# Eight plain products for the first feature tile of each FFN, a table written in eight pieces, and a queue clock in the emitter

## The chip, the cores and the metric

The kernel runs on one core of a Trainium2 chip. The metric is device time in microseconds (us). Five engines take part: TensorE (PE: matmuls, and weight loads that overlap them, PEld), VectorE (DVE), ScalarE (ACT), GpSimd (POOL) and SyncE (SP), which here only issues transfers. A transfer issued by SP goes to queue q1, one issued by POOL to q0; both use the same 16 DMA engines.

## The reference

One decoder layer over 1032 tokens (a prompt of 1024 and 8 single sample tokens), width 1024, in float32:

```
h <- LN1(alpha*h + 0.5*SwiGLU_1(h))            w_up 1024 x 5632, w_down 2816 x 1024
h <- LN2(alpha*h + merge(window attention(h), retention(h)) W_o)
h <- LN3(alpha*h + 0.5*SwiGLU_2(h))
SwiGLU(x) = (silu(x W_gate) * (x W_up)) W_down
```

The attention adds a relative-position bias to its scores; the kernel builds that table once. Both feed-forward networks (FFN 1 and FFN 2) have the same shape.

## The kernel before

**Precision.** A float32 operand is split in a high part (rounded to fp32r by a copy on ACT) and a low part (the rest, a subtraction on DVE). A product is three matmuls: high by high, high by low, low by high. For weights these are `w_hi` and `w_lo`, for tokens the two halves of the tiles `T`.

**Up stage.** FFN features are cut into 22 tiles `ft` of 128. For one tile the gate and the up weights are two row blocks; with two halves of the 1024 inputs they form a 2 x 2 block matrix, the tokens in two halves of 516 (columns) form another: b11, b21 are the input halves of the first 516 tokens (in `ya`, `yb`), b12, b22 those of the last. The kernel multiplies them in the Strassen-Winograd way: seven products (ft, 0) to (ft, 6) in place of eight. Each product is 4 k-steps x 3 parts x 2 column chunks = 24 matmuls of 258 columns. It needs sums of weight blocks (four additions on DVE in `sums`, into the tiles `st`) and sums of token blocks. The token operands T0 to T6 are made once for each FFN by `t_stage`: T0 = b11, T1 = b21 and T5 = b22 are plain (two ACT copies, two DVE subtractions); T2, T3, T4 and T6 are differences, each with two more DVE subtractions ahead, done in place in `ya` and `yb`, so that their order is bound. In the first seven steps of an FFN these operands are made while the products run. Products are accumulated in three PSUM pairs pr0 to pr2 (`pr`); `evac_p` empties them: copies on ACT, additions on DVE into the tiles `a`, then the gate (a tanh on ACT into `th`, then (th+1)*a on DVE), the product of gate and up part in `m`, its split in `ah` and `m`, and two stores to DRAM (`adr`).

Before, the first two tiles are interleaved: (0,0), (1,0), (0,1), (1,1), then (0,3), (0,2), (0,4), (0,5), (0,6), then the rest of tile 1, in FFN 1. In FFN 2, (0,0), (0,1), (1,0), (1,1) come first, which need only T0 and T1, while the last layer norm (`ln_last`) still works on the tokens from 768 on; `end_ln` waits for it.

**Down stage.** Features come back from DRAM in groups (`fetch_one`, transfers T<-adr of 1 MB); the first six are issued while the last up tile runs. A job is one 128 x 1024 row block of weights (two halves of 256 KB), used in 6 or 12 units over three token chunks. A unit's PSUM bank (`mb`, four in turn) is added to `ya` or `yb` by DVE.

**Weights.** Halves are loaded by SP in one fixed order into four buffers `raw`; the buffer is reloaded (`load`) once its last reader was issued. Eight slots hold split weights (`NSLOT`). `prep` issues the split of one half; `prep_ahead` calls it ahead of need, while slots are free and the half should have arrived by the emitter's clock.

**Order.** All instructions of an engine run in the order in which the program issues them. The emitter `E` keeps a model time for PE (`E.pe`) and for each other engine; `E.later` holds a piece of work until its model time; generators (side tasks) are resumed at model times; `need` issues a prep at once; while `env["busy"]` is set, `prep_ahead` does nothing. Model times set the order, nothing on the chip waits for them. A load's arrival by the model is

```
arrive[h] = E.pe + DMA_T          # DMA_T = 2.8
```

**Bias table.** `bias_tables` makes 8 rows of 256 values and writes each 128 times to DRAM with one POOL transfer (`scr<-rsb`, 8 x 128 x 256 values, 1 MB); the attention reads it back from 765 us on.

Of the kernel before, what the change touches and what calls it, by code (L numbers as in the profile page):

```python
# [40 lines left out]
DMA_T = 2.8  # L41
# [20 lines left out]
class Emit:  # L62


    def __init__(self, nc):
        self.nc = nc
        self.pe = 0.0
        self.eng = {"act": 0.0, "dve": 0.0, "pool": 0.0}
# [144 lines left out]
def build(tc, I, O):  # L213
# [3 lines left out]
    with ctx:  # L217
# [90 lines left out]
        def open_sa():  # L308
            p = ctx_open("sa", R)
            env["st"] = [p.tile([P, 4, P], F32, name=f"st{i}") for i in range(3)]  # L310
            env["a"] = [p.tile([P, HT], F32, name=f"a{i}") for i in range(4)]

        def open_ut():
            p = ctx_open("ut", L)
            env["th"] = p.tile([P, HT], F32, name="th")
# [28 lines left out]
        def ffn_units(p, r0):  # L344
# [12 lines left out]
            if p:  # L357
                pre = 2 * len(wrow)
                wrow.append(up[1])
                halves[pre] = halves[pre + 1] = 1  # L360
                src = {(1, 0): (pre, None), (1, 1): (pre + 1, None)}
            else:
                src = {(1, 0): (-1, None), (1, 1): (-2, None)}
            for ft in range(NF):
                h = 2 * len(wrow)
                wrow.extend((up[ft], up[ft] + 1))
                for k, n in enumerate((1, 1, 1, 2) if ft == 1 else (2, 2, 1, 2)):
                    halves[h + k] = n
# [6 lines left out]
            units.extend(dict(kind="P", p=p, c=0, ft=ft, i=i, jobs=[]) for ft, i in order)  # L375
# [46 lines left out]
        for ui, u in enumerate(units):  # L422
            u["ops"] = [quad_op[u["p"], u["ft"], u["i"]]] if u["kind"] == "P" else [o + i for o in (job_op[j] for j in u["jobs"]) for i in range(2)]
            for o in u["ops"]:
                lastu[o] = ui
# [42 lines left out]
        def prep():  # L468
# [6 lines left out]
            else:  # L475
                loaded(src)
                x = env["first"][-1 - src] if src < 0 else raw[src % NRAW]
# [4 lines left out]
            def lo():  # L482
                E.tt(w_lo[s], x, f(w_hi[s]), ALU.subtract, n=512)
                lo_of.pop(o, None)
                if not isinstance(src, str) and src >= 0:
                    used(src)
# [255 lines left out]
        env["first"] = [env["a"][i][:, 0:512].rearrange("p (k c) -> p k c", k=4) for i in (1, 3)]  # L742

        def first_half(t, row, h):
            ds(out=t, in_=half(I["w"][row].rearrange("p (k c) -> p k c", k=KD), h))

        for k in range(2):
            first_half(raw[k], wrow[0], k)
            for i in (0, 2):
                ds(out=env["yb" if k else "ya"][:, i:i + 2], in_=xd[:, 4 * k + i:4 * k + i + 2])  # L750
            first_half(env["first"][k], wrow[2], k)
        for h in range(4):
            arrive[h] = 0.0
            if h > 1:
                first_half(raw[h], wrow[1], h)
# [17 lines left out]
        def t_stage(i):  # L773
# [18 lines left out]
            elif i == 5:  # L792
                t_hl(5, b22)
            else:
                t_hl(6, sub(b11, b21, b11))

        def end_t(p):
# [6 lines left out]
            for fn in env.pop("held"):  # L804
# [26 lines left out]
        def start_u(p):  # L831
            env["held"] = []
            if p == 1:
                t_stage(1)
# [5 lines left out]
                env["a"] = [p.tile([P, HT], F32, name=f"a{i}") for i in range(2)] + [None] * 2  # L840
                open_pairs((1, 0, 2))

        def end_ln():

            E.force(list(lng.values()))
            env["a"][2:] = [env["ln"][:, i * HT:i * HT + HT] for i in (0, 1)]
            env["th"] = env["ln"][:, 2 * HT:3 * HT]

        def start_d(p):
# [8 lines left out]
            ds(out=env["ya"], in_=hres if p else xd[:, 0:4, :])  # L858
            alpha(env["ya"])
# [7 lines left out]
        def fetch_one():  # L867
# [3 lines left out]
            fstate["t"] = E.pe  # L871

# [34 lines left out]
        def bias_tables():  # L907
# [13 lines left out]
            dq(out=dst, in_=rsb.unsqueeze(1).to_broadcast([8, P, 256]))  # L921
# [361 lines left out]

        def evac_p(p, ft, i, bank):
            A = bank[:, :, 0:HC]
            v = lambda t: t.rearrange("p (c n) -> p c n", c=2)
            a1, a2, a5 = env["a"][ft % 2], env["a"][2], env["a"][3]

            def hold(fn):
                if "held" in env:  # L1290
                    env["held"].append(fn)
                else:
                    fn()

            def gate(a):

                def fn():
                    t = E.act(env["th"], a, AF.Tanh, scale=0.5, n=HT, after=E.eng["dve"])
                    env["glu"] = E.later(t, lambda: E.stt(a, env["th"], 1.0, a, ALU.add, ALU.mult, n=HT))

                hold(fn)

            if i in (0, 2, 3):
                E.act(v((a1, None, a2, a5)[i]), A, n=HT)
            elif i == 1:
                E.tt(v(a1), A, v(a1), ALU.add, n=HT)
                if ft != 1:
                    gate(a1)
            elif i == 4:
                E.tt(v(a5), A, v(a5), ALU.add, n=HT)  # L1310
                if "held" not in env:
                    E.do(env["glu"])
            elif i == 5:
                hold(lambda: E.do(env["glu"]))
                E.tt(v(a2), A, v(a2), ALU.add, n=HT)
                gate(a2)
            else:
# [4 lines left out]
                if ft == 0:  # L1322
                    gate(env["a"][1])
                t = E.act(ah, m, n=T, after=t)

                def lo():
                    t = E.tt(m, m, f(ah), ALU.subtract, n=T)

                    def out():
                        ds(out=adr[p, ft, :, 0:T], in_=f(ah))  # L1330
                        ds(out=adr[p, ft, :, T:2 * T], in_=m)

# [5 lines left out]
        def evac(u, bank):  # L1338
            kind, c = u["kind"], u["c"]
            n0, N = CH[c]  # L1340
            ps = None if kind == "P" else bank[:, :N]
            if kind == "P":
                evac_p(u["p"], u["ft"], u["i"], bank)
            elif kind == "down":
# [132 lines left out]
        def before(ui, u):  # L1477
            kind, c = u["kind"], u["c"]
            if kind == "P":
                p, ft, i = u["p"], u["ft"], u["i"]  # L1480
                o = u["ops"][0]
                if (ft, i) == (0, 0):
                    start_u(p)
                    if p:
                        for n in range(4):
                            need(o + n)
# [5 lines left out]
                    env["busy"] = True  # L1492
                    env["aside"] = lambda: (need(o + 4), need(o + 5))
                elif not p and (ft, i) == (1, 0):
                    need(o + 1)
                    t_stage(1)
                elif not p and (ft, i) == (1, 1):
                    need(o)
                    need(o + 1)
                elif ft == 0 and i > 1:  # L1500
                    if p and i == 3:
                        end_ln()
                        t_stage(3)
                    need(o)
                    if i < 6:
                        t_stage({3: 2, 2: 4, 4: 5, 5: 6}[i])
                    else:
                        end_t(p)
                        env["busy"] = False
                if ft == 0 and i in tready:  # L1510
                    E.pe = max(E.pe, tready.pop(i))
# [41 lines left out]
        def product(u, bank):  # L1553

            o = u["ops"][0]
            need(o)
            s, x = slot_of[o], TT[u["i"]]
            fresh = u["i"] in (0, 1, 3)
            for k in range(4):
                wh, wl = w_hi[s][:, k, :], w_lo[s][:, k, :]  # L1560
                for n, (w, lo) in enumerate(((wh, 0), (wh, 2 * T), (wl, 0))):
                    for c in range(2):
                        a = lo + k * HT + c * HC
# [182 lines left out]
```

## Time and profile before

| | |
|---|---|
| median of three runs | 2272.85 us (2272.41 to 2273.28) |
| profiled execution, own time | 2270.69 us |
| its span, first to last instruction | 2268.9 us |
| mean granted TensorE clock | 0.980 |
| DMA over the span | 254.88 MB, mean 112 GB/s |

In a timeline each line is: start, duration, engine, line of the kernel, instruction, output<-input, shape, count; in brackets the idle time of that engine just before, and what ended it. `raw<-in_w_dram` is a weight half, `T<-adr` a fetch of stored features, `w_hi` and `w_lo` are the parts of a split weight. A clock below 1.00 in a stage means that TensorE was granted less than its full clock there. Line 105 is the helper of all DVE operations, 101 of all activations, 83 of all matmuls.

### The profile page before, as it was taken

How to read it: one execution, taken by the hardware profiler on the slowest of the kernel's cores; microseconds unless marked ns; L12 is line 12 of the kernel's file. 1: busy time of each engine (PE TensorE's matmuls, PEld its weight loads, DVE VectorE, ACT ScalarE, POOL GpSimd, SP SyncE). 2: the span in 40 equal slices, each digit the busy share in tenths (PEclk: the TensorE clock that was granted, in tenths of full speed). 3: DMA queues.
4: the chain of work that ended last, by engine and by line, in shares of the span. 5: the costliest groups of instructions: out<-in, count | busy, mean ns of one | idle time of the engine just before them, and what ended most of it. 6: DMA issues, size and time to landing. Idle time of an engine off the chain costs nothing.

```text
span 2268.9 us, 38235 instructions
## 1 busy us (share of the span) xinstructions
PE 2169.8 (96%) x15333; PEld 2134.0 (94%) x15333; DVE 1377.2 (61%) x2575; ACT 772.8 (34%) x1481; POOL 227.9 (10%) x283
## 2 busy tenths in 40 slices
PE   6899999989999899999999999987999999989996
PEld 5899999989999889999989999987999999989996
DVE  7666666654334887555665847778666666543337
ACT  4343433321111576111233434544434434311113
POOL 1100000001002444111110201011000000010003
PEclk9999999999999999999999999998999999999998
DMA  3522332266330210111154344532223322484212
GB/s 124 130 102 102 112 108 104 94 235 259 122 103 28 64 41 30 47 39 39 57 178 144 131 130 131 186 108 84 102 101 113 108 104 100 173 316 145 85 42 75
DMA packets 105571, 254.88 MB, mean 112 GB/s; under 512 B 13370, under 2 KB 17170, under 8 KB 98978
## 3 DMA queue, kind: packets, MB, share of 16 engines
q1 hardware_dynamic: 104546, 251.36, 32.0%
q0 software_dynamic: 848, 1.09, 0.5%
q8 instruction: 120, 1.97, 0.4%
q14 instruction: 57, 0.47, 0.1%
HBM read 196.00 MB, written 57.45 MB: 112 GB/s over the span
## 4 chain that ended last, share of the span: by engine, by line
PE 79%; DVE 10%; DMA 5%; ACT 2%; issue 2%; POOL 1%; SPq 0%; DVEq 0%; POOLq 0%; ACTq 0%
PE mb L83 41%; PE pr L83 36%; DMA raw<-in_w_dram 5%; DVE w_lo L105 2%; PE sb L83 2%; DVE ya L105 1%; DVE T L105 1%; DVE yb L105 1%; DVE ln L105 1%; DVE zt L105 1%; ACT w_hi L101 1%; DVE rt L105 1%; ACT T L101 0%; POOL pt L121 0%; PE sb L91 0%
## 5 line engine op out<-in xcount | busy, mean ns | idle before, releaser
L83 PE MATMUL mb<-T,w_hi 128*128 128x384 f32 (+1 forms) x3936 | 930.8, 324 | 14.2 <-DVE yb L105 14.2
L83 PE MATMUL pr<-T,w_hi 128*128 128x258 f32 x4928 | 809.3, 287 | 35.6 <-ACT w_hi L101 12.9
L83 PEld LDWEIGHTS pr<-T,w_hi 128*128 128x128 f32 x4928 | 691.3, 192 | 41.1 <-ACT w_hi L101 14.4
L83 PEld LDWEIGHTS mb<-T,w_hi 128*128 128x128 f32 x3936 | 680.3, 189 | 20.2 <-DVE yb L105 15.1
L83 PE MATMUL mb<-T,w_lo 128*128 128x384 f32 (+1 forms) x1968 | 632.4, 321 | 0.0
L83 PE MATMUL pr<-T,w_lo 128*128 128x258 f32 x2464 | 504.2, 286 | 9.3 <-DVE w_lo L105 9.0
L101 ACT ACTIVATE w_hi<-raw 128x512 fp32r<-128x512 f32 x498 | 303.1, 624 | 478.0 <-PE mb L83 424.6
L105 DVE TENSOR_TENSOR w_lo<-raw,w_hi 128x512 fp32r<-128x512 f32 x498 | 350.9, 729 | 125.6 <-ACT w_hi L101 124.8
L83 PEld LDWEIGHTS pr<-T,w_lo 128*128 128x128 f32 x2464 | 389.4, 192 | 11.4 <-DVE w_lo L105 11.4
L83 PEld LDWEIGHTS mb<-T,w_lo 128*128 128x128 f32 x1968 | 372.1, 189 | 0.0
L105 DVE SCALAR_TENSOR_TENSOR yb<-mb,yb 128x384 f32<-128x384 f32 (+1 forms) x144 | 73.5, 514 | 136.3 <-PE mb L83 136.0
L105 DVE SCALAR_TENSOR_TENSOR ya<-mb,ya 128x384 f32<-128x384 f32 (+1 forms) x144 | 74.1, 515 | 134.3 <-PE mb L83 134.1
L101 ACT ACTIVATE w_hi<-st 128x512 fp32r<-128x512 f32 x132 | 82.5, 628 | 116.0 <-PE pr L83 59.6
L105 DVE TENSOR_TENSOR a<-pr,a 128x516 f32<-128x516 f32 x88 | 61.2, 696 | 99.5 <-PE pr L83 99.4
L125 POOL TENSOR_SCALAR ya<-ya 128x384 f32<-128x384 f32 (+1 forms) x24 | 11.6, 483 | 871.1 <-DMA ya<-hres 449.6
L105 DVE TENSOR_TENSOR w_lo<-st,w_hi 128x512 fp32r<-128x512 f32 x132 | 86.9, 684 | 0.0
L101 ACT ACTIVATE th<-a 128x516 f32<-128x516 f32 x44 | 28.0, 635 | 122.4 <-DVE a L105 121.6
L101 ACT ACTIVATE a<-pr 128x516 f32<-128x516 f32 x88 | 52.8, 601 | 40.4 <-PE pr L83 40.3
L105 DVE TENSOR_TENSOR ln<-pr,ln 128x516 f32<-128x516 f32 x44 | 30.6, 695 | 54.0 <-PE pr L83 54.0
L83 PE MATMUL mb<-o_hi,w_hi 128*128 128x384 f32 (+1 forms) x192 | 61.9, 322 | 0.0
L83 PE MATMUL mb<-g_lo,w_hi 128*128 128x384 f32 (+1 forms) x192 | 61.4, 320 | 0.0
L83 PE MATMUL mb<-g_hi,w_lo 128*128 128x384 f32 (+1 forms) x192 | 61.2, 319 | 0.0
(316 smaller groups left out, 2069.8 us busy)
## 6 DMA issues: line engine op xcount, KB each, us to landing
raw<-in_w_dram SPq DMA_DIRECT2D x502, 256.0 KB, 2.9
T<-adr SPq DMA_DIRECT2D x44, 1032.0 KB, 6.5
adr<-ya SPq DMA_DIRECT2D x44, 516.0 KB, 2.7
adr<-ah SPq DMA_DIRECT2D x22, 516.0 KB, 3.1
adr<-m SPq DMA_DIRECT2D x22, 516.0 KB, 4.1
out_yp_dram<-zt SPq DMA_DIRECT2D x16, 256.0 KB, 2.0
ya<-in_x_dram SPq DMA_DIRECT2D x2, 1032.0 KB, 8.9
yb<-in_x_dram SPq DMA_DIRECT2D x2, 1032.0 KB
```

Of the source, the lines that this page charges most:

```text
L83: self.nc.tensor.matmul(out=out, lhsT=lhsT, rhs=rhs, start=start, stop=stop, **kw)
L101: self.nc.scalar.activation(out=out, in_=in_, func=func, scale=scale, **kw)
L105: getattr(self.nc.vector, fn)(**kw)
L125: self.nc.gpsimd.tensor_scalar(out=out, in0=a, scalar1=s, scalar2=1.0, op0=ALU.mult, op1=ALU.mult)
```

## The change

It has three parts.

1. The first feature tile of each FFN is computed by eight plain products without weight sums. They stand in four units of kind "C", each of two products accumulated in one PSUM pair: C0 (gate, first token half: T0 and T1), C1 (up, first half: T0, T1), C2 (gate, second half: b12 and b22), C3 (up, second half). b12 gets an operand of its own (`t_stage(7)`, in the buffer that later holds T6); T5 is b22. The order is C0, C1, (1,0), (1,1), C2, C3, (1,3), (1,2), (1,4), (1,5), (1,6), then tile 2, in both FFNs. The differences are staged from C1 on in FFN 1, from C3 on in FFN 2. The four weight halves of tile 0 keep their slots from C0 to C3. `evac_c` empties the units: a copy, a gate, or a product with the gated tile; the split and the store of tile 0 wait (`held_ut`) until the buffers are free, and gates in FFN 2 wait (`held_th`) for `end_ln`. A fifth tile `a` is added, and `th` moves. The two weight halves of tile 1 that were loaded an additional time for the interleaving are loaded once.
2. The bias table is written by eight POOL transfers of 128 KB, one after another, 8 us of model time apart.
3. The emitter has a clock of the load queue: each load of a half (0.262 MB), fetch and store (1.057 MB) and the reload of the residual (2.114 MB) adds its size at 0.38 MB/us. A half's arrival is the later of that clock and of DVE's model time, plus 2.0 us.

The diff, cut to its core:

```
-DMA_T = 2.8
+DMA_T = 2.0
+DMA_R = 0.38
...
+    def dma(self, mb):
+        self.queue = max(self.queue, self.pe) + mb / DMA_R
+        return self.queue + DMA_T
...
-            order = [(0, 0), (0, 1), (1, 0), (1, 1)] if p else [(0, 0), (1, 0), (0, 1), (1, 1)]
-            order += [(0, i) for i in (3, 2, 4, 5, 6)]
-            order += [(ft, i) for ft in range(NF) for i in range(7) if (ft, i) not in order]
...
+            order = [(1, 0), (1, 1)]
+            order += [(1, i) for i in (3, 2, 4, 5, 6)]
+            order += [(ft, i) for ft in range(2, NF) for i in range(7)]
+            quad_op[p, 0] = [o + k for o in [job_op[add_job(up[0] + i)] for i in range(2)] for k in range(2)]
...
+            first = [dict(kind="C", p=p, c=0, ft=0, i=i, jobs=[]) for i in range(4)]
+            rest = [dict(kind="P", p=p, c=0, ft=ft, i=i, jobs=[]) for ft, i in order]
+            units.extend(first[:2] + rest[:2] + first[2:] + rest[2:])
...
-                arrive[h] = E.pe + DMA_T
+                arrive[h] = max(E.dma(0.262), E.eng["dve"] + 0.7 + DMA_T)
...
+            elif i == 6:
+                t_hl(6, sub(b11, b21, b11))
             else:
-                t_hl(6, sub(b11, b21, b11))
+                t_hl(6, b12)
...
             ds(out=env["ya"], in_=hres if p else xd[:, 0:4, :])
+            E.dma(2.114)
...
             fstate["t"] = E.pe
+            E.dma(1.057)
...
-            dq(out=dst, in_=rsb.unsqueeze(1).to_broadcast([8, P, 256]))
+            for h in range(8):
+                dq(out=dst[h:h + 1], in_=rsb[h:h + 1].unsqueeze(1).to_broadcast([1, P, 256]))
+                yield E.pe + 8.0
...
+        def evac_c(p, i, bank):
+            A = bank[:, :, 0:HC]
+            if i == 0:
+                E.act(v(env["a"][0]), A, n=HT)
+            elif i == 2:
+                gate(env["a"][4], A)
+            else:
+                def fn():
+                    a = env["a"][i // 2 * 4]
+                    if i == 1:
+                        gate(a)
+                    E.do(env["glu"])
+                    E.tt(v(a), A, v(a), ALU.mult, n=HT)
+                hold("held_th", fn)
...
+            if kind == "C":
+                p, i = u["p"], u["i"]
+                o = quad_op[p, 0][0]
+                env["busy"] = True
+                if i == 0:
+                    start_u(p)
+                    if p:
+                        for k in range(6):
+                            need(o + k)
+                        env["aside"] = lambda: (need(o + 6), need(o + 7))
+                    else:
+                        need(o)
+                        t_stage(0)
+                        t_stage(7)
+                        need(o + 1)
+                        t_stage(1)
+                        need(o + 2)
+                        need(o + 3)
+                elif i == 1 and not p:
+                    need(o + 4)
+                    need(o + 5)
+                    t_stage(5)
+                    t_stage(3)
+                elif i == 2:
+                    if p:
+                        end_ln()
+                        t_stage(7)
+                        t_stage(5)
+                    else:
+                        t_stage(4)
+                elif i == 3:
+                    if p:
+                        t_stage(3)
+                        t_stage(2)
+                    else:
+                        need(o + 8)
...
+            else:
+                xs = [TT[i] for i in ((0, 1), (6, 5))[u["i"] // 2]]
```

For tile 1, T2 is staged ahead of (1,0) in FFN 1 (in FFN 2 with C3), T6 ahead of (1,3) in FFN 1, T4 ahead of (1,3) and T6 ahead of (1,2) in FFN 2.

More of the change, by code (lines that the diff above doesn't have):

```diff
@@ L476, in prep @@
                 loaded(src)
-                x = env["first"][-1 - src] if src < 0 else raw[src % NRAW]
+                x = raw[src % NRAW]
             s = slot_of[o] = free_slots.pop(0)
@@ L484, in lo @@
                 lo_of.pop(o, None)
-                if not isinstance(src, str) and src >= 0:
+                if not isinstance(src, str):
                     used(src)
@@ L740, in build @@
         xd = I["x"]
[L742 to L751, printed above, removed]
         for h in range(4):
+            ds(out=raw[h], in_=half(I["w"][wrow[h // 2]].rearrange("p (k c) -> p k c", k=KD), h))
             arrive[h] = 0.0
-            if h > 1:
-                first_half(raw[h], wrow[1], h)
+            for i in (0, 2) if h < 2 else ():
+                ds(out=env["yb" if h else "ya"][:, i:i + 2], in_=xd[:, 4 * h + i:4 * h + i + 2])
         state["load"] = 4
@@ L839, in start_u @@
                 env["st"] = [p.tile([P, 4, P], F32, name=f"st{i}") for i in range(3)]
[L840 removed]
+                env["a"] = [p.tile([P, HT], F32, name=f"a{i}") for i in range(2)] + [None] * 3
                 open_pairs((1, 0, 2))
@@ L1281, in o_split, with v, hold, gate @@
                 t = E.tt(env["o_lo"][:, k, :N], src, f(oh), ALU.subtract, n=N)
+        def v(t):
+            return t.rearrange("p (c n) -> p c n", c=2)
+        def hold(k, fn):
+            if k in env:
+                env[k].append(fn)
+            else:
+                fn()
+        def gate(a, src=None):
+            if env.get("glu"):
+                E.do(env["glu"])
+            src = v(a) if src is None else src
+            t = E.act(v(env["th"]), src, AF.Tanh, scale=0.5, n=HT, after=E.eng["dve"])
+            env["glu"] = E.later(t, lambda: E.stt(v(a), v(env["th"]), 1.0, src, ALU.add, ALU.mult, n=HT))
+        def evac_c(p, i, bank):
[9 more added lines that the diff above has]
+                        gate(a)
+                    E.do(env["glu"])
+                    E.tt(v(a), A, v(a), ALU.mult, n=HT)
+                hold("held_th", fn)
+            if i < 3:
+                return
+            def out():
+                m, ah = env["m"][0], env["ah"][0]
+                for k, a in ((0, env["a"][0]), (HT, env["a"][4])):
+                    t = E.act(ah[:, k:k + HT], a, n=HT)
+                    E.tt(m[:, k:k + HT], a, f(ah)[:, k:k + HT], ALU.subtract, n=HT, after=t)
+                ds(out=adr[p, 0, :, 0:T], in_=f(ah))
+                ds(out=adr[p, 0, :, T:2 * T], in_=m)
+            hold("held_ut", out)
         def evac_p(p, ft, i, bank):
             A = bank[:, :, 0:HC]
-            v = lambda t: t.rearrange("p (c n) -> p c n", c=2)
             a1, a2, a5 = env["a"][ft % 2], env["a"][2], env["a"][3]
[L1289 to L1301, printed above, removed]
             if i in (0, 2, 3):
@@ L1553, in product @@
         def product(u, bank):
[L1555 to L1563, printed above, removed]
-                        E.mm(bank[:, c, 0:HC], w, x[:, a:a + HC], fresh and k == 0 and n == 0, k == 3 and n == 2, skip_group_check=True)
-                if k < 3:
-                    prep_ahead()
-                    E.run()
+            if u["kind"] == "P":
+                xs = [TT[u["i"]]]
+                fresh = u["i"] in (0, 1, 3)
+            else:
+                xs = [TT[i] for i in ((0, 1), (6, 5))[u["i"] // 2]]
+                fresh = True
+            for j, (o, x) in enumerate(zip(u["ops"], xs)):
+                need(o)
+                s = slot_of[o]
+                for k in range(4):
+                    wh, wl = w_hi[s][:, k, :], w_lo[s][:, k, :]
+                    end = k == 3 and j == len(xs) - 1
+                    for n, (w, lo) in enumerate(((wh, 0), (wh, 2 * T), (wl, 0))):
+                        for c in range(2):
+                            a = lo + k * HT + c * HC
+                            E.mm(bank[:, c, 0:HC], w, x[:, a:a + HC], fresh and j + k + n == 0, end and n == 2, skip_group_check=True)
+                    if not end:
+                        prep_ahead()
+                        E.run()
         env["nu"] = 0
```

100 lines of the change are left out of this document (50 added, 50 removed).

## The prediction

> **What bounds the kernel now.** I read the page first, then busy time by stage, then the timeline, the chain and the waits wherever TensorE falls short.
>
> ```profile
> PE 2169.8 (96%) x15333; PEld 2134.0 (94%) x15333; DVE 1377.2 (61%) x2575; ACT 772.8 (34%) x1481; POOL 227.9 (10%) x283
> ...
> PE   6899999989999899999999999987999999989996
> ...
> PEclk9999999999999999999999999998999999999998
> ```
>
> TensorE (PE) is busy 96% of the span. So more products cost time everywhere but in its gaps, and a gain can come only from the gaps. Busy time by stage (PE, weight loads, VectorE (DVE), ScalarE (ACT), GpSimd (POOL), clock, DMA share, GB/s) shows where they are:
>
> ```profile
> 8.40:20.00 11.60, 8.72 (x51) 7.85 (x52) 9.89 (x12) 7.72 (x12) 1.70 (x3) 0.83 0.89 347
> 20.00:76.00 56.00, 42.49 (x289) 40.16 (x290) 43.43 (x57) 23.60 (x35) 0.00 (x0) 0.88 0.22 71
> ...
> 108.50:120.00 11.50, 5.11 (x29) 5.11 (x30) 5.36 (x9) 3.25 (x6) 0.00 (x0) 0.70 0.44 135
> 120.00:490.00 370.00, 370.00 (x3062) 370.00 (x3061) 228.64 (x342) 144.65 (x236) 0.00 (x0) 1.00 0.32 113
> 490.00:510.00 20.00, 13.35 (x67) 13.03 (x66) 8.55 (x15) 2.32 (x3) 0.00 (x0) 0.74 0.78 293
> ...
> 1505.00:1580.00 75.00, 52.93 (x356) 50.14 (x355) 61.59 (x76) 33.39 (x49) 13.58 (x16) 0.84 0.21 68
> 1580.00:1984.00 404.00, 404.00 (x3351) 404.00 (x3350) 251.98 (x377) 158.72 (x259) 0.00 (x0) 1.00 0.33 114
> 1984.00:2004.00 20.00, 14.25 (x82) 13.93 (x81) 9.67 (x17) 2.96 (x4) 0.00 (x0) 0.83 0.79 295
> ```
>
> Undisturbed up stages have no gap: 370.00/3062 = 0.1208 us a matmul, so 2.90 us a product of 24. Five places fall short: the two FFN starts, 108 to 120, and the two turns from up to down. There the clock drops too (0.70 to 0.88), so a gap costs more than its length. The change touches all five. I cost them one by one.
>
> **1. First tile, FFN 1.** Times here are starts; the bracket is the idle time before, and who ended it.
>
> ```profile
> 7.68 1.16 ACT L101 ACTIVATE T<-ya 128x516 fp32r<-128x516 f32 x2 [3.56 <-DMA ya<-in_x_dram]
> 13.07 2.37 DVE L105 TENSOR_TENSOR ya<-ya 128x1032 f32<-128x1032 f32 x2
> 15.43 2.38 DVE L105 TENSOR_TENSOR T<-ya,T 128x1032 fp32r<-128x1032 f32 x2
> 17.44 2.01 ACT L101 ACTIVATE T<-yb 128x1032 fp32r<-128x1032 f32 x2
> 18.55 0.51 PE L83 MATMUL pr<-T,w_hi 128*128 128x258 f32 x2 [1.90 <-ACT T L101]
> 24.08 0.70 DVE L105 TENSOR_TENSOR a<-pr,a 128x516 f32<-128x516 f32 x1 [3.18 <-PE pr L83]
> 75.88 0.70 DVE L105 TENSOR_TENSOR m<-pr,a 128x516 f32<-128x516 f32 x1 [2.20 <-PE pr L83]
> ```
>
> Now the first two tiles are 14 products. They run from about 8.4 to 75.7 (the evacuation of the last starts at 75.88): 67.3 us for 40.6 us of work. The cause is in the two DVE rows. A token operand that is a difference costs DVE 2.37 (subtract) + 2.38 (low part) = 4.75 us; a plain one 2.38; a product is consumed in 2.90. Four of seven operands are differences, and DVE is busy 43.43 of 56 us.
>
> Afterwards there are 15 products: +2.90 us for each FFN, 5.8 in all, fully on the path. DVE loses four weight sums and three w_lo of tile 0 (7 x 0.69 = 4.8 us) and two evacuation adds (1.4), and gains one plain operand (2.4). The first six products now need only plain operands T0 and T1. Two weight loads go, and T1 no longer queues behind a difference, so I put it at 16 to 17 instead of 17.44. C0 then ends near 21.5 (its like ended before 24.08). C1, (1,0) and (1,1) add four products: 33.1.
>
> Then comes a new wait. (1,1) is accumulated in pr0, C2 needs pr0, and the add that empties it is queued on DVE behind T5 (2.4), T3 (4.75), the gate of C1 (1.4), T2 (4.75) and two w_lo (1.4). From 22.7, after the first evacuation, that list with small waits ends at 38. So C2 waits about 5 us, and some 2 us go to the low clock (the gaps of parts 3 and 4 cost 1.5 to 2 us more than their length). C2 and C3 end near 52; (1,3) and (1,2), with 0.8 for pr2 that C3 has just written, at 58.5; three more products 67.2; DVE is then nearly full with T6, two sums and the stores, for which I add 2. End 69.2: **gain 6.5 us**. Bounds: no wait at all, 8.4 + 43.5 = 51.9, a gain of 24; all waits as now and one more product, a loss of 2.9.
>
> **2. First tile, FFN 2.**
>
> ```profile
> 1505.24 0.64 PE L83 MATMUL pr<-T,w_hi 128*128 128x258 f32 x4
> 1528.07 2.09 ACT L101 ACTIVATE yb<-yb,lnp 128x264 f32<-128x264 f32 x4
> 1531.17 0.80 PE L83 MATMUL pr<-T,w_hi 128*128 128x258 f32 x2 [6.46 <-ACT T L101]
> 1579.98 0.70 DVE L105 TENSOR_TENSOR ya<-pr,a 128x516 f32<-128x516 f32 x1 [2.18 <-PE pr L83]
> ```
>
> Now 14 products take 1505.2 to 1579.8, 74.6 us. Four of them cover the last layer norm; then PE idles 6.46 us. Afterwards six cover it, ending near 1529.6 where four ended at 1524.7. But two more w_lo (1.3) stand in front of the norm on DVE, and behind it two tanh and a gate stand before T7, so C2 starts near 1534.5, not 1531.2. C2 and C3 last till 1548.4 (some 2.2 us at the low clock). On DVE the queue is T3, T2 (9.5), then C3's gate and product; T3's ACT part stands behind the tanh that waits for C2. That frees pr2, which (1,3) needs, at about 1552.7: a wait of 4.3. From there five products (14.5), low clock 2.1, a bank just written 0.8, a full DVE 2 as in FFN 1, and 1.2 for a weight behind T6's low part give 1573.3. **Gain 6.5 us**, with the same bounds (24 and -2.9).
>
> **3. The bias table in pieces.**
>
> ```profile
> raw<-in_w_dram SPq DMA_DIRECT2D x502, 256.0 KB, 2.9
> ...
> 86.51 1.12 POOL L921 DMA_DIRECT2D scr<-rsb  x1 [76.27 <-ACT rsb L101]
> ...
> scr<-rsb POOLq DMA_DIRECT2D x1, 1024.0 KB, 25.0
> ...
> q0 software_dynamic: 65, 0.23, 48.3%
> ...
> 96.76 15.36 DMA raw<-in_w_dram
> ...
> 112.21 0.69 DVE L105 TENSOR_TENSOR st<-raw,raw 128x512 f32<-128x512 f32 x1 [8.84 <-DMA raw<-in_w_dram]
> 114.89 1.23 PE L83 MATMUL pr<-T,w_hi 128*128 128x258 f32 x4 [6.45 <-ACT a L101]
> ```
>
> One write of 1 MB occupies its engines for 25.0 us, at 48.3% of 16 engines (window 90 to 95): about eight, as many as its outermost index. A weight half issued at 96.76 lands after 15.36 us, its sums start at 112.21, and PE idles 6.45 us. 29 matmuls in 11.5 us where 95 fit: 66 x 0.1208 = 8.0 us lost. A piece is an eighth. Spread over 16 engines it holds each for 25.0 x 8/16/8 = 1.6 us; on a single engine it holds that for 25.0. I take the first: the nearest row is the weight half, 128 rows as well, which lands 256 KB in 2.9 us where one of the eight engines here moved 128 KB in 25.0. And a tile bears a half that is 1.6 us late: of DVE's 8.84 us of waiting PE lost 6.45. **Gain 8.0**, bounds 8.0 and the loss of the second rival below. Seven more POOL issues (7 x 1.12) delay only the scaling of yb behind them, due at 490.
>
> The Trainium skill, page "DMA: Bandwidth & Descriptors", section "Why a DMA increments its semaphore by 16 and not by 1", has the engine count follow from the slowest dimension that is not 1. That gives 8 for the one write, which 48.3% bears out, and 16 for a piece, whose 128 copies would then lead; by it the sum stands, and no run here shows a piece yet. Read by the outermost index alone, a piece has one engine, which is the rival.
>
> **4. The clock of the load queue.** It issues nothing on the chip. It moves the prep of weights (w_hi on ACT, w_lo on DVE) later in the instruction order, to when the half should have landed. PE's part is the same.
>
> ```profile
> T<-adr SPq DMA_DIRECT2D x9, 1032.0 KB, 10.7
> ...
> 484.48 15.50 DMA raw<-in_w_dram
> ...
> 494.95 0.69 DVE L105 TENSOR_TENSOR w_lo<-raw,w_hi 128x512 fp32r<-128x512 f32 x1 [4.60 <-ACT w_hi L101]
> 495.56 0.69 DVE L105 TENSOR_TENSOR m<-pr,a 128x516 f32<-128x516 f32 x1
> ...
> 500.06 0.63 ACT L101 ACTIVATE w_hi<-raw 128x512 fp32r<-128x512 f32 x1 [2.12 <-DMA raw<-in_w_dram]
> 500.72 0.69 DVE L105 TENSOR_TENSOR w_lo<-raw,w_hi 128x512 fp32r<-128x512 f32 x1 [1.51 <-ACT w_hi L101]
> 501.33 1.94 DVE L105 SCALAR_TENSOR_TENSOR yb<-mb,yb 128x384 f32<-128x384 f32 x4
> 501.94 1.01 PE L83 MATMUL mb<-T,w_hi 128*128 128x384 f32 x2 [6.65 <-DVE yb L105]
> ...
> 1995.24 1.01 PE L83 MATMUL mb<-T,w_hi 128*128 128x384 f32 x2 [5.75 <-DVE yb L105]
> ```
>
> At the turn to the down stage 1 MB fetches are on the queue, and a weight half needs 15.50 us where the old rule says 2.8. Its prep is already in the streams: DVE waits with a w_lo, and four finished banks behind it wait too, so PE idles 6.65 us. By order of prep this weight is for the fourth job, some 38 us on (12 units of 6 matmuls each, three jobs): nothing needed it yet. By the new arithmetic its arrival is put (6 x 1.057 + 1.057 + 4 x 0.262)/0.38 + 2 = 24 us after the first fetch, against 26 by the trace (473.7 to 500). So the wait shrinks to some 2 us, about what the four banks bear. Lost now: 20 - 58 x 0.177 - 9 x 0.1208 = 8.7 us for a 6.65 us gap; for the 5.75 us gap likewise about 7.4. I take **7.5 and 6.5**; bounds for both 0 and 16. A half whose w_lo is later is reloaded later, behind more fetches; three finished jobs cover that, and if that cover went, a wait of up to 15.50 us would return.
>
> Sum: 6.5 + 6.5 + 8.0 + 7.5 + 6.5 = 35 us against the profiled execution's 2270.69 (span 2268.9 and 1.8 around it): 2235.7. The median is 2.2 above that execution, so **2238 us**.
>
> **Rivals.** *The starts give nothing*: DVE stays the limit, and the bank waits of C2 and (1,3) double (5 + 4.3 us more). For it: DVE 61.59 of 75 us. 2238 + 13 = 2251. *One engine for each piece*: 8 x 8 + 25.0, some 89 us with a slow engine, four tiles losing 8.0 each instead of one: 2238 + 4 x 8.0 = 2270, no change. *The turn stays as it is*, since w_lo is still put in front of the evacuations: 2238 + 14 = 2252. *Slower*: in the undisturbed up stage the clock, which adds 1.057/0.38 = 2.8 us for each tile's store, puts a prep so late that PE waits once a tile: 40 x 2.8 = 112, 2350 us; it decides from 35/40 = 0.9 us a tile. Against it:
>
> ```profile
> L101 ACT ACTIVATE w_hi<-raw 128x512 fp32r<-128x512 f32 x75 | 46.5, 620 | 1.4 <-DMA raw<-in_w_dram 0.8 <-PE pr L83 0.6
> ```
>
> From 120 to 490 ACT waits 0.8 us in all for weights, and eight slots put a prep up to eight products (23 us) ahead.
>
> **How the numbers follow.** Forecast 0.62; starts give nothing 0.15; turn stays 0.13; one engine 0.05; slower 0.05. Faster (over 0.2%, which is about what a measurement can tell here): 0.90, same 0.05, slower 0.05. The range 2222 to 2256 holds the first three with their spread: down to 16 us below the forecast, if the starts lose only half of the waits left to them and the turns all; up to the two rivals near 2252 and a little. What lies above is 0.10.
>
> **What would show it.** PE's gap at 108 gone, and q0 in short bursts; at the turns yb evacuations before the w_lo that waits for a load; 15 products ending near 69 and 1573; waits of C2 for a DVE add and, in FFN 2, of (1,3) for pr2. Wrong I would be if raw loads took over 10 us after 86, if ACT or DVE still waited for loads at the turns, or if PE had gaps between 120 and 490.

## The result and the profile after

The changed kernel takes 2250.07 us (median of four runs, 2248.05 to 2251.36) against 2272.8 us: ratio 0.9899, 95% interval 0.9882 to 0.9916. That is 23 us faster, 12 us less than the 35 us of the prediction's sum. The profiled execution after took 2248.05 us, its span is 2246.0 us.

The first rows of the profile after: busy time of each engine, then TensorE's busy share in 40 slices.

```profile
PE 2165.3 (96%) x15381; PEld 2133.5 (95%) x15381; DVE 1369.7 (61%) x2561; ACT 772.4 (34%) x1477; POOL 236.0 (11%) x290
...
PE   7979999999999899999999999997999999999996
```

The 48 matmuls more than before (15381 against 15333) are the two additional products. The third slice (112 to 168 us), a 9 before, is a 7 now; the slices at the two turns, 8 before, are 9 now.

To place the difference I cut both spans at the same seven events: the evacuation of (1,6) in FFN 1 (the row `m<-pr,a` at 75.88 before, 73.54 after), the first `mb` matmul of the turn, the first matmul of LN1, the first product of FFN 2, the evacuation of (1,6) there (1579.98 before, 1564.47 after), the second turn, the end.

| stage | before | after | change | predicted |
|---|---|---|---|---|
| start of FFN 1 | 75.9 | 73.5 | -2.3 | -6.5 |
| rest of up stage 1 (has the bias write) | 415.0 | 423.1 | **+8.1** | **-8.0** |
| turn 1 and down stage 1 | 232.5 | 223.4 | -9.2 | -7.5 |
| layer norms, attention, retention | 781.8 | 776.6 | -5.3 | 0 |
| start of FFN 2 | 74.7 | 67.9 | -6.8 | -6.5 |
| rest of up stage 2 | 405.1 | 405.8 | +0.7 | 0 |
| turn 2 and down stage 2 | 283.8 | 275.8 | -8.0 | -6.5 |
| span | 2268.9 | 2246.0 | -22.9 | -35 |

Busy time by stage after (length of the window, then PE, weight loads, DVE, ACT and POOL with their instructions, clock, DMA share, GB/s):

```profile
20.00:73.50 53.50, 42.24 (x328) 41.63 (x327) 38.46 (x46) 22.00 (x31) 0.00 (x0) 0.92 0.16 52
100.00:160.00 60.00, 47.46 (x361) 47.04 (x360) 28.42 (x44) 17.07 (x28) 4.61 (x9) 0.89 0.67 90
160.00:480.00 320.00, 320.00 (x2649) 320.00 (x2648) 199.44 (x298) 126.23 (x207) 0.00 (x0) 1.00 0.30 103
490.00:510.00 20.00, 20.00 (x139) 19.69 (x138) 13.26 (x23) 5.13 (x8) 0.00 (x0) 1.00 0.89 358
```

At the turn (490 to 510) TensorE is full at clock 1.00, where it had 13.35 of 20 us at 0.74. Between 100 and 160 us it has 361 matmuls where the undisturbed rate would give some 497. That stretch holds the loss, and the chain of waits, the timeline and the queue view of the changed kernel show what stands in it:

```profile
102.94 35.21 DMA raw<-in_w_dram x2
```

```profile
91.16 0.55 POOL L928 DMA_DIRECT2D scr<-rsb  x1 [80.65 <-ACT rsb L108]
91.79 9.22 POOL L132 TENSOR_SCALAR yb<-yb 128x384 f32<-128x384 f32 x12
101.07 3.68 POOL L928 DMA_DIRECT2D scr<-rsb  x7
...
126.40 1.23 PE L90 MATMUL pr<-T,w_hi 128*128 128x258 f32 x4 [6.01 <-ACT a L108]
140.93 1.23 PE L90 MATMUL pr<-T,w_hi 128*128 128x258 f32 x4 [6.52 <-ACT a L108]
```

```profile
q0 software_dynamic: 48, 0.13, 89.6%
...
raw<-in_w_dram SPq DMA_DIRECT2D x2, 256.0 KB, 29.7
```

```profile
q0 software_dynamic: 384, 1.05, 32.1%
...
scr<-rsb POOLq DMA_DIRECT2D x8, 128.0 KB, 17.4
```

The first of these fences is from the chain, the second from the timeline, and the last two are the queue from 105 to 110 us and from 60 to 160 us. Two things differ from what was planned. The pieces are not 8 us apart: the first goes out at 91.16, and the other seven within 3.68 us from 101.07. Only the emitter's model spaced them, and POOL, with nothing to wait for, issued them one behind the other. And each is dear: from 105 to 110 us q0 alone fills 89.6% of all 16 engines, and from 60 to 160 us it takes 32.1% of them, which is 32.1 us of all 16. Two weight halves need a median of 29.7 us in place of 2.9, and TensorE waits 6.01 and 6.52 us.

The engine count agrees with the rule of the Trainium skill, page "DMA: Bandwidth & Descriptors", section "Why a DMA increments its semaphore by 16 and not by 1": a piece whose 128 copies lead takes 16 engines, and 89.6% bears it out. What was wrong is what those engines then need for a row.

### The profile page after: what moved, and what is told of

Read it like the earlier page. It is cut to its first block, busy times and chain, and to the rows that moved or that the text cites. A ratio compares the mean times of both kernels' runs of the same rounds, so it can differ in the third digit from the quotient of the medians.

```text
span 2246.0 us, 38320 instructions
## 1 busy us (share of the span) xinstructions
PE 2165.3 (96%) x15381; PEld 2133.5 (95%) x15381; DVE 1369.7 (61%) x2561; ACT 772.4 (34%) x1477; POOL 236.0 (11%) x290
## 4 chain that ended last, share of the span: by engine, by line
PE 83%; DVE 8%; DMA 3%; ACT 3%; issue 2%; POOL 1%; SPq 0%; ACTq 0%; DVEq 0%; POOLq 0%
PE mb L90 43%; PE pr L90 37%; DMA raw<-in_w_dram 3%; PE sb L90 2%; DVE T L112 1%; DVE w_lo L112 1%; DVE ya L112 1%; DVE yb L112 1%; ACT w_hi L108 1%; DVE zt L112 1%; ACT T L108 1%; DVE ln L112 1%; PE mb L98 1%; DMA ya<-in_x_dram 0%; POOL pt L128 0%
## 5 line engine op out<-in xcount | busy, mean ns | idle before, releaser
L90 PE MATMUL mb<-o_lo,w_hi 128*128 128x384 f32 (+1 forms) x192 | 61.2, 319 | 0.0
```

The lines of the kernel that those rows point to most:

```text
L90: self.nc.tensor.matmul(out=out, lhsT=lhsT, rhs=rhs, start=start, stop=stop, **kw)
```

## The experiments on the bias write

Two questions stood: are the pieces themselves the loss, and has another part of the change made any write dearer? Each ratio below is to the kernel before as measured beside that run; its medians there lay between 2271.1 and 2274.7 us, so medians of different runs compare only to some 2 us.

**One write again** (`one_write`).

```
-            for h in range(8):
-                dq(out=dst[h:h + 1], in_=rsb[h:h + 1].unsqueeze(1).to_broadcast([1, P, 256]))
-                yield E.pe + 8.0
+            dq(out=dst, in_=rsb.unsqueeze(1).to_broadcast([8, P, 256]))
```

> The changed kernel with the bias table written by one transfer again. Theory P: the pieces are what lost time between 100 and 160 us; PE lost 139 matmuls there (16.8 us) where the one write cost 8.0, so this kernel comes out 8 to 9 us below the changed one, near 2242, with a single gap of 6 to 7 us. Rival Q: the gaps at 120 and 134 come from the queue clock, which lets a prep wait for a late load, and not from the form of the write; then two gaps stay and the time is 2250.

Measured 2248.21 us, ratio 0.9893 (0.9874 to 0.9911). Neither expectation held: there is one gap and not two, but the time is far from 2242. The pieces cost some 2 us over the single write (between 100 and 160 us TensorE has 380 matmuls here against 361, which is 2.3 us), and the two intervals overlap. But the single write itself had become dearer. Timeline of `one_write`:

```profile
91.70 1.12 POOL L927 DMA_DIRECT2D scr<-rsb  x1 [81.09 <-ACT rsb L108]
...
116.19 0.69 DVE L112 TENSOR_TENSOR st<-raw,raw 128x512 f32<-128x512 f32 x1 [14.84 <-DMA raw<-in_w_dram]
118.88 1.23 PE L90 MATMUL pr<-T,w_hi 128*128 128x258 f32 x4 [12.46 <-ACT a L108]
```

One gap of 12.46 us, where the kernel before had 6.45. The write starts 5.2 us later (91.70 against 86.51), so the loads beside it land later too, while the products that want them come 2 us sooner. The first tile does this and not the clock: with the clock alone (`clock_only`, below) the write starts at 86.46 and the gap is 8.05 us, with the first tile alone (`first_tile_only`) it starts at 97.93 and the gap is 12.94.

**The same, later** (`late_write`): the task wakes at 560 and not at 60 of the emitter's time.

```
-            yield 60.0
+            yield 560.0
```

> As one_write, but the table is made and written some 500 us later in model time, in the down stage, where weights are split three jobs ahead. Theory P: a raw load that takes 15 us then delays nothing; PE has no gap between 80 and 490, and the time is 16 us below the changed kernel, near 2234. Rival R: the write only moves its gap into the down stage (a wait of 6 to 7 us for w_lo or for the evacuation behind it): 2242 as with one write.

Measured 2235.16 us (2233.34 to 2237.37), ratio 0.9841 (0.9821 to 0.986), the lowest median of all that were run (by its ratio it is level with `spaced` and `rows16` below). Its windows, and the write at its new place:

```profile
100.00:160.00 60.00, 60.00 (x499) 60.00 (x498) 37.50 (x57) 23.98 (x39) 0.00 (x0) 1.00 0.29 104
...
560.00:620.00 60.00, 60.00 (x378) 59.32 (x377) 22.92 (x43) 6.70 (x11) 1.12 (x1) 1.00 0.38 93
```

```profile
598.72 1.12 POOL L927 DMA_DIRECT2D scr<-rsb  x1 [92.58 <-ACT rsb L108]
...
scr<-rsb POOLq DMA_DIRECT2D x1, 1024.0 KB, 25.6
```

499 matmuls against 361 in the same 60 us: 138 x 0.1202 = 16.6 us that the write in pieces costs in the changed kernel. In the down stage, where a weight half serves 6 or 12 units, the same write takes 25.6 us and TensorE stays full.

**An earlier single write** (`early_write`): one write, woken at 52.

```
-            yield 60.0
+            yield 52.0
```

> The changed kernel with one bias write, its task woken at 52 and not at 60 of the planner's time, so that the write is issued some 7 us earlier, about 84.5 us and not 91.70 after the span's start. Theory L (the write takes 24 to 25 us beside the weight loads wherever it starts, the loads beside it land when it ends, and the new first tile only makes the write start 5 us later against loads that are wanted 2 us sooner): the gap of TensorE behind it falls from 12.5 to about 5 us, and the time from 2248.2 to about 2241 (2239 to 2243). Rival T (the new first tile takes away the spare time of the loads, and the gap does not depend on where the write starts): 12 us and 2247 to 2250.

Measured 2240.92 us, ratio 0.9864 (0.9846 to 0.9882). Timeline of `early_write`:

```profile
82.55 1.12 POOL L927 DMA_DIRECT2D scr<-rsb  x1 [72.17 <-ACT rsb L108]
103.45 1.23 PE L90 MATMUL pr<-T,w_hi 128*128 128x258 f32 x4 [4.01 <-ACT a L108]
```

The write starts 9.1 us earlier than in `one_write`, and the gap falls from 12.46 to 4.01, as theory L put it. So what a write costs here depends on the moment at which it starts.

**Pieces across the heads** (`rows16`): still eight pieces of 128 rows, but each takes 16 copies of all eight heads, so its source is 8 partitions, not one.

```
-                dq(out=dst[h:h + 1], in_=rsb[h:h + 1].unsqueeze(1).to_broadcast([1, P, 256]))
+                dq(out=dst[:, 16 * h:16 * h + 16], in_=rsb.unsqueeze(1).to_broadcast([8, 16, 256]))
```

> The changed kernel with the table still written in eight pieces, but each piece holds 16 of the 128 copies of all eight heads, so that its rows are read from 8 partitions of rsb and not from one. Sizes and number of the pieces (128 rows of 1 KB each) stay. Theory S (the source partition is the price: 16 engines that read one partition need about 0.53 us per row where the single write needed about 0.2): the share of the write's queue over the span falls from 1.5% back to about 0.5%, the stretch in which all 16 engines are full shrinks from about 31 us to about 12 to 15, the raw loads beside it land in under 15 us instead of 29.7, and TensorE loses under 8 us between 100 and 160 us instead of 16.8: 2240 us (2236 to 2245). Rival N (it is the number of pieces, or that they stand back to back on the queue): the queue's share stays at 1.5% and the time at 2248 to 2252. Rival B (engine time falls, but the load that feeds the next weights is behind the write all the same, as with one write): 2246 to 2250, with one gap of about 12 us.

Measured 2238.01 us, ratio 0.9842 (0.9824 to 0.986). Page, waits from 80 to 200 us, and queue from 60 to 200 us of `rows16`:

```profile
q0 software_dynamic: 960, 1.09, 0.9%
```

```profile
PE pr L90 <- ACT a L108: 2.9, 1, 2.9
```

```profile
q0 software_dynamic: 640, 1.05, 13.0%
...
scr<-rsb POOLq DMA_DIRECT2D x8, 128.0 KB, 12.1
```

13.0% of 140 us is 18.2 us of all 16 engines, not 32.1. The time hit; the engine time fell less than expected (0.9% of the span, not 0.5), and a half beside it still took 16.5 us. The number of pieces and their being back to back are the same as in the changed kernel, so the price lay in how a piece is cut. This cut changes the source partitions and the place in DRAM that a piece writes, and with them the number of engines that a piece has. The queue lines of the last section tell the engines apart from the other two; the source and the place were not told apart.

**Pieces really spaced** (`spaced`): single-head pieces as in the change, each behind a one-element copy on POOL that reads the weights prepared last.

```
+            tick = p.tile([1, 1], F32, name="tick")
             for h in range(8):
+                s = slot_of[state["prep"] - 1]
+                nc.gpsimd.tensor_copy(out=tick, in_=f(w_hi[s])[0:1, 0, 0:1])
                 dq(out=dst[h:h + 1], in_=rsb[h:h + 1].unsqueeze(1).to_broadcast([1, P, 256]))
```

> The changed kernel with its eight single-head pieces, each behind a one-element copy on GpSimd that reads the weights prepared last, so that the pieces really start one after another, some 8 us apart, and not seven of them back to back when GpSimd has run ahead. Theory S (each piece costs about 31/8 = 3.9 us of all 16 engines wherever it stands; a raw load that falls on one is late by at most that, which the 8 us of buffer between load and use cover): no gap of TensorE above 2 us between 80 and 200 us, and the prediction's own step comes true: 2250 less 14 to 17 = 2233 to 2237. Rival N (each piece holds its own queue of loads up for its whole landing of 6.3 us, and the lateness adds up): the same loss in more, smaller waits: 2246 to 2251.

Measured 2236.9 us, ratio 0.9831 (0.9809 to 0.9854). Windows, queue (60 to 200 us) and two of the pieces of `spaced`:

```profile
100.00:120.00 20.00, 20.00 (x168) 20.00 (x167) 14.69 (x19) 7.88 (x13) 9.75 (x15) 1.00 0.78 84
120.00:140.00 20.00, 20.00 (x168) 20.00 (x167) 12.54 (x19) 8.00 (x13) 2.13 (x5) 1.00 0.75 150
```

```profile
q0 software_dynamic: 384, 1.05, 21.1%
...
scr<-rsb POOLq DMA_DIRECT2D x8, 128.0 KB, 6.9
```

```profile
114.17 0.72 POOL L930 COPY tick<-w_hi 1x1 f32<-1x1 f32 x1 [4.86 <-ACT w_hi L108]
...
123.68 0.38 POOL L930 COPY tick<-w_hi 1x1 f32<-1x1 f32 x1 [8.30 <-ACT w_hi L108]
```

The engines spend almost the same, 21.1% of 140 = 29.5 us, but in portions 6 to 10 us apart that land in 6.9 us each (the median), and TensorE loses nothing. So the step that failed had two faults, and mending either is nearly enough: pieces 1.8 times cheaper in one burst, or dear ones apart.

## The experiments on the other parts

**The first tile alone** (`first_tile_only`): the changed kernel with one write and the old rule of arrival.

```
-                arrive[h] = max(E.dma(0.262), E.eng["dve"] + 0.7 + DMA_T)
+                arrive[h] = E.pe + 2.8
```

> The eight plain products alone: one bias write, arrivals by the old rule (2.8 us after issue). Theory: both starts gain what they gained in the changed kernel (2.3 and 6.8 us), and nothing else moves: 2272.8 - 9 = 2264. Rival: the 5.3 us that the stretch from the first layer norm to FFN 2 gained come from the first tile too (other alignment of the side tasks): 2258. Rival: the starts gain by the clock: 2270.

Measured 2277.56 us, ratio 1.0023 (1.0011 to 1.0034): slower than before, which none of the expectations held. Timeline of `first_tile_only`:

```profile
43.25 1.23 PE L90 MATMUL pr<-T,w_hi 128*128 128x258 f32 x4 [8.55 <-DVE a L112]
57.37 0.71 PE L90 MATMUL pr<-T,w_hi 128*128 128x258 f32 x4 [0.88 <-DVE a L112]
69.06 1.23 PE L90 MATMUL pr<-T,w_hi 128*128 128x258 f32 x4 [5.65 <-ACT a L108]
```

With the old rule a preparation whose load has not landed stands on ACT, which waits 3.24 us for its sums, and a bank's copy stands behind it: TensorE waits 5.65 us at 69.06, where the changed kernel has 1.82. The start of FFN 1 ends at 80.1, 4.2 us later than before; the write costs a gap of 12.94 us; only FFN 2's start gains, 3.6 us.

**The clock alone** (`clock_only`): the kernel before with part 3 of the change.

> The kernel before with the queue clock alone. Theory: the two turns gain 9 and 8 us, and the middle stretch its 5.3, since preps no longer block DVE and ACT there: 2272.8 - 22 = 2250.5. Rival: the middle is no work of the clock: 2256. Rival: the turns gained by the order of the first tile, not by the clock: 2270.

Measured 2252.64 us, ratio 0.9914 (0.9898 to 0.993). It has nearly the whole gain: -9.2 from the first turn on, -7.9 from the second. It also fills a stretch of 160 us of the retention. Windows of the kernel before (first row), `first_tile_only` (second) and `clock_only` (third):

```profile
940.00:1100.00 160.00, 157.09 (x1053) 154.75 (x1052) 96.37 (x246) 24.59 (x47) 28.39 (x39) 1.00 0.13 42
```

```profile
950.60:1110.60 160.00, 156.60 (x1045) 154.30 (x1044) 94.53 (x237) 24.27 (x46) 27.51 (x38) 1.00 0.13 42
```

```profile
931.50:1091.50 160.00, 160.00 (x1086) 158.79 (x1085) 98.21 (x252) 25.75 (x49) 29.53 (x39) 1.00 0.13 42
```

Some 3 us of gaps go with the clock and stay without it; in all ten kernels with the clock TensorE is full in this stretch, in the four without it 156.6 to 157.1 of 160 us. That is a part of the -5.3 us in the middle. The rest is not settled: over the whole middle the profiled executions with the clock differ among themselves (774.0 in `clock_late` to 782.2 in `spaced`, against 780.7 to 784.4 without it).

**The parts without the write's loss.** Three more kernels hold the late write (`yield 560.0`): the kernel before, the first tile without the clock, the clock without the first tile.

> The kernel before with nothing changed but the moment of its one bias write, some 500 us later. Theory A (the write costs the kernel before the 8.0 us that the prediction read from its trace): 2272 - 8 = 2264 (2262 to 2266); then the new first tile without the clock, 2263.1 with the late write, is worth 0 to 2 us, against 8 us beside the clock (2243.2 to 2235.2). Rival B (a part of the 8 us returns as other waits, or the write costs as much at its new place): 2267 to 2272, and the first tile is then worth 4 us or more without the clock too.

> The kernel with the new first tile alone, the old arrival of loads and one bias write, this some 500 us later. Theory A (the parts add up; with the early write the gap was 12.94 us): 2277.6 - 12.9 = 2264.7 (2262 to 2267), which leaves the first tile a gain over the kernel before only through its second start. Rival D (without the clock the new first tile's conversions stand in ScalarE's queue ahead of loads that have not landed at other places too, so that the write's removal uncovers other waits): 2269 to 2275.

> The kernel before with the clock of the queue and with its one bias write some 500 us later; the first tile is the old one. Theory A (the three parts add up: in the run with the clock alone the write cost a gap of 8.05 us): 2252.6 - 8 = 2244.6 (2243 to 2247), and the new first tile is then worth the rest to 2235.2, some 9 us, -2.3 at the first start and -6.8 at the second. Rival Z (the new first tile gains nothing of its own once the write is out of the way): 2234 to 2238.

| with the late write | us | ratio to before, interval |
|---|---|---|
| kernel before (`before_late`) | 2264.52 | 0.9957 (0.9945 to 0.9969) |
| first tile (`first_late`) | 2263.12 | 0.9964 (0.9954 to 0.9974) |
| clock (`clock_late`) | 2243.17 | 0.9869 (0.9846 to 0.9892) |
| first tile and clock (`late_write`) | 2235.16 | 0.9841 (0.9821 to 0.986) |

All three came out where the parts add up. The 8.0 us that the prediction read from the trace of before as the price of the write is there: moving nothing but the write gives 2264.52 us, by its ratio 7.0 to 12.5 us less. Without the clock the first tile is worth nothing measurable (0.9964 against 0.9957), with it some 6 to 8 us (0.9841 against 0.9869). These two intervals overlap a little, so I add the profiles: from `clock_late` to `late_write` the start of FFN 1 is 2.7 us shorter (76.12 to 73.47) and that of FFN 2 6.7 us (75.27 to 68.55). The two spans differ by only 2.0 us (2234.2 and 2232.2), since the profiled execution of `clock_late` is its fastest by 6.5 us and its middle is 4.7 us shorter than that of `late_write`. Without the clock the second start is shorter too (69.66 in `first_late` against 75.69 in `before_late`), the first longer (79.25 against 78.03). So that the first tile needs the clock is likely, but not shown clear of noise.

**The starts.** After the change the third product of the first tile in FFN 1 waits 8.56 us, not the predicted 5. Timeline of the changed kernel:

```profile
37.82 0.68 DVE L112 TENSOR_TENSOR st<-raw,raw 128x512 f32<-128x512 f32 x1
...
40.35 1.29 DVE L112 TENSOR_TENSOR w_lo<-st,w_hi 128x512 fp32r<-128x512 f32 x2
41.55 0.69 DVE L112 TENSOR_TENSOR a<-pr,a 128x516 f32<-128x516 f32 x1
42.30 1.23 PE L90 MATMUL pr<-T,w_hi 128*128 128x258 f32 x4 [8.56 <-DVE a L112]
```

Ahead of the addition that frees pr0 stand the four weight sums of (1,3) and (1,2) and two w_lo, 3.7 us from 37.82 to 41.55: `stages([], [1] if p else [1, 2, 3])` issues them before (1,1). The prediction's list had no sums, and ended at 38. `late_sums` lets them come with their own products:

```
-                        stages([], [1] if p else [1, 2, 3])
+                        stages([], [1])
```

> The changed kernel with the weight sums for (1,3) and (1,2) of the first block no longer prepared ahead of (1,1), but where their own products come. Nothing else moves. Theory H (the third product of the first tile waits 8.56 us for an addition on VectorE because 3.7 us of weight sums and w_lo stand ahead of it): that wait falls to about 4.9 us, (1,3) and (1,2) wait no more than about 1 us for their own sums, and the time falls by 2.7 to 3.7 us from 2250: 2246 to 2247.5. Rival M (the sums are only moved into the next bottleneck, since VectorE is full there): the 8.56 us falls and about as much appears as waits of (1,3) and (1,2): 2249 to 2251.

Measured 2249.24 us, ratio 0.9891 (0.9874 to 0.9908): no gain that can be told from the changed kernel. Timeline of `late_sums`:

```profile
37.87 1.23 PE L90 MATMUL pr<-T,w_hi 128*128 128x258 f32 x4 [4.83 <-DVE a L112]
...
60.18 0.80 PE L90 MATMUL pr<-T,w_lo 128*128 128x258 f32 x2 [4.59 <-DVE w_lo L112]
```

The first wait falls by 3.73 us, as reckoned, and a new one of 4.59 us for a w_lo behind T4's two subtractions takes its place: the rival held. `both_starts` has the late write, this edit, and in FFN 2 the operands one product later:

```
-                        stages([6] if not p else [4], [2] if p else [5, 6])
+                        stages([6] if not p else [2], [2] if p else [5, 6])
...
-                        stages([6], [4, 5])
+                        stages([], [4])
+                        stages([4], [])
                     elif i == 4 and p:
+                        stages([], [5])
+                        stages([6], [])
...
-                        t_stage(2)
```

> The changed kernel with one bias write some 500 us later, the weight sums of the first block moved as in the last run, and in the second block T2 taken at (1,3), T4 and the weights of (1,4) at (1,2), T6 and those of (1,5) at (1,4), each one product later than in the changed kernel. With the late write alone it is 2235.2. Theory H (each wait at the two starts is work that stands in VectorE's and ScalarE's queues one product too early): 3 to 3.7 us at the first start and 3 to 5.8 at the second: 2226 to 2229 us. Rival M (these engines are full from the start to (1,6), so a wait moved returns at the next product): 2232 to 2236.

Measured 2238.09 us (2232.85 to 2242.16), ratio 0.9843 (0.9817 to 0.9868): not better than `late_write`. In the profiles its first start is 5.4 us longer (78.90 against 73.47, with a wait of 6.40 us for a w_lo), its second 3.5 us shorter (65.07 against 68.55). The second half of the edit did what was expected at the low end, the first did the opposite. The late write with the edit of FFN 2 alone was not run.

## Why the prediction was right or wrong, point by point

**What bounds the kernel** held: the gains came from TensorE's gaps at the turns and starts, and TensorE still is 96% busy.

**The bias table in pieces** is the step that failed: the stage lost 8.1 us in place of gaining 8.0. The term "Spread over 16 engines it holds each for 25.0 x 8/16/8 = 1.6 us" measured 4.0 us (32.1 us of all engines in eight pieces). It took over the price of a row from the single write, which reads eight partitions, and the nearest row that it named was a weight half; neither reads one partition alone, as each piece does. And "a tile bears a half that is 1.6 us late" took the pieces to come one by one; seven came in 3.68 us. The rival "one engine for each piece" was wrong too (the engines were 16), though it had a loss where a loss came. A second cause was in no step: the new first tile makes the write start 5 us later, so that even one write costs a gap of 12.46 us. Of the 16.6 us that the pieces cost, one write would have cost 14.3 (380 matmuls against 499), so the pieces added 2.3 us where they were to take the whole loss away. The size of the prize, 8.0 us, was right.

**The first tile, FFN 1** was mis-sized: -2.3 in place of -6.5. Of the 4.2 us, 3.6 are the third product's wait (8.56 against 5) behind sums that the list of DVE's work had left out. `late_sums` shows that putting them later frees nothing: the wait returns at a later product, as the rival "the starts give nothing" said of this start.

**The first tile, FFN 2** was right: -6.8 against -6.5, with the waits in the places named:

```profile
1524.97 0.80 PE L90 MATMUL pr<-T,w_hi 128*128 128x258 f32 x2 [3.80 <-ACT T L108]
...
1544.11 1.20 PE L90 MATMUL pr<-T,w_hi 128*128 128x258 f32 x4 [4.51 <-DVE ln L112]
```

(1,3) waits 4.51 us for pr2, forecast 4.3. What neither step on the first tile saw is that such a gain may lean on the clock: without it the first start came out longer, by 4.2 us in `first_tile_only` and 1.2 in `first_late`.

**The clock** was right in its mechanism and somewhat small: -9.2 and -8.0 against -7.5 and -6.5. At the turn of the changed kernel the bank evacuations now stand before the w_lo, and a late load delays only ACT:

```profile
500.43 1.48 DVE L112 SCALAR_TENSOR_TENSOR yb<-mb,yb 128x384 f32<-128x384 f32 x3
501.82 0.68 DVE L112 TENSOR_TENSOR w_lo<-raw,w_hi 128x512 fp32r<-128x512 f32 x1
...
505.19 0.63 ACT L108 ACTIVATE w_hi<-raw 128x512 fp32r<-128x512 f32 x1 [5.12 <-DMA raw<-in_w_dram]
```

The wait of some 2 us that the prediction had allowed for was not left on TensorE, so the rival "the turn stays as it is" did not come. That the clock also fills gaps in the retention was not forecast. The rival "slower", a wait for every tile, did not come: from 160 to 480 us TensorE is full (320.00 of 320.00).

Of the signs by which the prediction said that it would be wrong, all came: raw loads took a median of 29.7 us behind the pieces, TensorE had gaps that end at 126.40 and 140.93, and ACT waited 5.12 us for a load at the first turn. The first two belong to the pieces; the third cost TensorE nothing.

That the total lies inside the range is in part luck, for errors of opposite sign make it up: +16.1 (the stage of the write) and +4.2 (start 1) against -5.3 (middle) and -3.2 (turns), with +0.3 in the rest. Without the -5.3 and -3.2 the time would have been 2258.6 us, above the 2256 of the range. And 2250 us is about what two rivals gave that did not come, "the starts give nothing" as a whole (2251) and "the turn stays as it is" (2252): only the stages tell them from what happened.

## What to carry to other kernels

A background transfer that is cut in pieces is only spread if something on the chip spaces the pieces; an emitter's model time does not, on an engine that has nothing to wait for. Before cutting, look for a stage where the whole transfer is free: moving it by one constant gave 7.0 to 12.5 us in the kernel before, where the pieces were to give 8.0, and some 15 us in the changed one (2250.07 to 2235.16). And an arrival rule that sees the queue (some 20 us alone) was worth more than the new order of products, which gave nothing measurable without it.

## What the runs showed of the hardware

Rows of 1 KB that are all read from one partition by 16 engines cost far more engine time than the same rows from eight partitions: 32.1 us of all 16 engines for 1024 rows (0.50 us a row on its engine) against 18.2 us (0.28) when each piece took all eight, and 10.7 us (0.17) in the single write, which ran on eight engines (10.7% of the window from 60 to 160 us in the kernel before). I had expected the bytes alone to count.

The bytes moved in a window show that much of this engine time is waiting. These are the queue from 105 to 110 us of `rows16`, the same window of `one_write`, and the first piece of `rows16`, which stood alone (90 to 95 us):

```profile
q0 software_dynamic: 149, 0.22, 84.5%
```

```profile
q0 software_dynamic: 56, 0.23, 46.8%
```

```profile
q0 software_dynamic: 80, 0.13, 25.8%
```

In 5 us the pieces of `rows16` moved 0.22 MB with 84.5% of the engines and the single write 0.23 MB with 46.8%: more engines on the same eight partitions did not move more. The single-head pieces moved 0.13 MB in those 5 us with 89.6%. So on the same partitions more engines only waited longer for a row, and how the piece was cut set the rate. A piece of `rows16` took 1.3 us of all 16 engines when it stood alone (25.8% of 5 us) and some 2.4 us in the burst; a single-head piece took about 4 us either way (31.4% of 13 us alone in `spaced`). Whether the source or the written place sets the rate stays open.
